# The convolution product of an attention layer: eight block products or seven

## The chip, the cores and the metric

The kernel runs on one core of one Trainium2 chip. The metric is the device time of one launch in microseconds (us), the median of several runs. The engines of the core run side by side, each through its own list of instructions in order: TensorE (PE; its weight loads are PEld), VectorE (DVE), ScalarE (ACT), GpSimd (POOL), and SyncE (SP), which here issues nearly all DMA transfers.

## The reference

One layer over 1024 latent tokens and 256 context tokens, model width 1024: a half-step SwiGLU network, then two token mixers side by side (a gated short convolution and an attention with 8 query heads and 2 key/value heads), merged by sigmoid gates, then a second SwiGLU network. What matters here is the mixing:

```python
y_conv_l = conv_branch(bg_l, cg_l, vc_l, conv_w[layer])          # (1024 tokens, 1024 channels)
o_l = latent_attention(q_l, k_all, v_all)
x = x + ml[5] * merge_branches(y_conv_l, o_l, gt_l, w_branch_conv[layer], w_branch_attn[layer], w_out[layer])

def merge_branches(y_conv, o_attn, gate_logits, w_bc, w_ba, w_out):
    g_conv, g_attn = jnp.split(jax.nn.sigmoid(gate_logits), 2, axis=-1)
    return (g_conv * (y_conv @ w_bc) + g_attn * (o_attn @ w_ba)) @ w_out
```

The change concerns `y_conv @ w_bc`, a product of 1024 x 1024 by 1024 x 1024, and its gate.

## The kernel before

All matmuls of weight carry precision in two parts: a float32 value is split into a high part (rounded to the matmul's format by ScalarE, `CAST`) and a low part (the difference, by VectorE or GpSimd, `TENSOR_TENSOR`). `split` (line 197) does it. A product of two values is then three matmuls: high by high, high by low, low by high (`mm3`). Latents lie with channels on the 128 partitions, so y is 8 blocks k of 128 channels by 1024 tokens, and the tokens are two chunks of 512, C0 and C1. y waits in DRAM (`yd`), the gates too (`gcd`), and the gated result goes to `zd`.

**The product with y.** `conv_inputs(ch)` (line 1523) loads the 8 blocks of a chunk and splits them. `conv_weights(j)` (line 1515) loads the 1024 x 128 columns of w_bc for output block j (512 KB, tile `raw`, 3 buffers) and splits them into `wc`. `conv_out(ch, j)` (line 1543) runs 8 x 3 = 24 matmuls of 512 columns into a PSUM bank, multiplies by the gate on VectorE (`g<-g,ps`) and stores to `zd`. That is 8 blocks x 2 chunks x 24 = 384 matmuls; each weight block is loaded and split twice.

**The attention.** There are 16 units (8 heads x 2 chunks), class `Unit` (line 1579). A unit has four query tiles; `scores` runs, for each, nine matmuls (three of 256 columns on `kc`, six of 512 on `kl`), VectorE takes the maxima (`m<-ps`, `nm`), and ScalarE the exponentials (`pc`, `pl`). The unit after it, `seconds` (line 1648) turns the previous unit's probabilities: ten steps of four transposes (`pt<-ident,pl`), a split on ScalarE and VectorE (`pts`), and three value matmuls (into `po` or `ps`). In the middle of it, `inverse` (line 1635) has VectorE take a reciprocal (`rinv`), and GpSimd's own DMA queue writes it to DRAM (`rinvd`) and reads it back spread over the partitions (`rrow`); GpSimd then scales the unit's output (`q<-q,rrow`).

**What sets the order.** Four products of C0 stand around the last head unit (its normalised, rotated heads are the tiles `xb`; `hsw` is a GpSimd helper of them; the transposes are `pt<-ident,xb`) and around unit 0's scores. The rest is in `fillers` (line 1705), a generator that the loop over units (line 1724) advances ten steps a unit: in most steps three matmuls of a block product stand in TensorE's list among the attention's. A scheduler then sets each engine's list from the program's order, its own estimates and the free tile slots; only instructions marked as pinned keep their written order. Short-lived 128 x 512 tiles all share 11 slots (`ttile`, line 116).

Of the kernel before, what the change touches and what calls it, by code (L numbers as in the profile page):

```python
# [9 lines left out]
F32 = mybir.dt.float32  # L10
F32R = mybir.dt.float32r
# [7 lines left out]
P = 128  # L19
D = 1024  # L20
KD = D // P
# [17 lines left out]
W_BUFS = 4  # L39
# [8 lines left out]
SLOT = 1024  # L48
# [3 lines left out]
def tile_dit_layer(  # L52
# [70 lines left out]
    def ps_s(n=512):  # L123
        return psum.tile([P, 512], F32, tag="s", name=uniq("ps"), bufs=5)[:, :n]
# [72 lines left out]
    def split(src, hi, lo, lo_eng=None, hi_eng=None):  # L197

        if hi_eng is dve:
            dve.tensor_copy(out=hi, in_=src)  # L200
        else:
            act.copy(out=hi, in_=src)
        (lo_eng or dve).tensor_sub(out=lo, in0=src, in1=hi.bitcast(F32))

    def load_parts(name, src, pinned=False):

        t = atile(name, (P, 2, 512), F32R)
        raw = t[:, 1].bitcast(F32)
        load(raw, src, pinned)
        split(raw, t[:, 0], t[:, 1])  # L210
        return t
# [280 lines left out]
    class Winograd:  # L492
# [21 lines left out]
        def keep(self, i, k, src, lo_eng=None):  # L514

            t = atile(f"r{i}", (P, 2, 512), F32R)
            split(src, t[:, 0], t[:, 1], lo_eng)
            self.r[i][k] = t
# [992 lines left out]
                )  # L1511

    ys, w_conv = {}, {}

    def conv_weights(j, lo_eng=None, tags=("wl", "wl")):
        raw = wpool.tile([P, SLOT], F32, tag="raw", name=uniq("raw"), bufs=3)
        hi, lo = (wpool.tile([P, SLOT], F32R, tag=tag, name=uniq("wc"), bufs=W_BUFS) for tag in tags)
        v = lambda t: t[:].rearrange("p (k n) -> p k n", k=KD)
        load(v(raw), w_bc[0][:, j * P : (j + 1) * P].rearrange("(k p) n -> p k n", p=P))
        split(raw[:], hi[:], lo[:], lo_eng)  # L1520
        w_conv[j] = v(hi), v(lo)

    def conv_inputs(ch, ks=range(KD), pinned=True):
        ys.setdefault(ch, []).extend(load_parts("y", yd[k, :, ch[1] : ch[1] + 512], pinned=pinned) for k in ks)

    before, N_UNITS = iter(()), 13
    for i, h in enumerate(heads()):
        run(before, 1)
        if i == N_UNITS - 1:
            conv_inputs(C0)  # L1530
        run(h, 1)
        if i == 0:
            for k in range(4):
                mix.part_second(k)
        if i == N_UNITS - 1:
            for j in range(2):
                conv_weights(j, tags=("wh", "wl"))
        run(before)
        before = h
    run(before, 1)  # L1540
    run(late_steps)

    def conv_out(ch, j):

        w, o = w_conv.pop(j), ch[1]
        ps, g = ps_s(), ttile("g")
        sp.dma_start(out=g, in_=gcd[j, :, o : o + 512])
        terms = [(w[0][:, k], w[1][:, k], ys[ch][k][:, 0], ys[ch][k][:, 1]) for k in range(KD)]
        for k in range(KD - 1):
            mm3(ps, terms, k, k + 1)  # L1550
            yield
        mm3(ps, terms, KD - 1)
        dve.tensor_mul(out=g, in0=g, in1=ps)
        sp.dma_start(out=zd[j, :, o : o + 512], in_=g)
        yield

    run(conv_out(C0, 0))
    conv_weights(2)
    run(before)
    run(conv_out(C0, 1))  # L1560
    conv_weights(3)

    o_parts = [None] * NQ

# [129 lines left out]
    u = units[0]  # L1697
    u.begin()
    for qt in range(4):
        u.scores(qt)  # L1700
        if qt < 3:
            run(conv_out(C0, 2 + qt))
            conv_weights(4 + qt)

    def fillers():

        for j in range(5, KD):
            conv_weights((j + 2) % KD, pool)
            yield from conv_out(C0, j)
            yield  # L1710
        for ks in ((0, 1), (2, 3), (4, 5), (6, 7)):
            conv_inputs(C1, ks, pinned=False)
            yield
            yield
        for j in range(KD):
            if j < KD - 2:
                conv_weights(j + 2, pool)
            yield from conv_out(C1, j)
            yield

    rest, fill = seconds(), fillers()
# [190 lines left out]
```

## Time and profile before

| | |
|---|---|
| median of 3 runs | 2631.08 us (2630.84 to 2632.65) |
| span of the profiled execution, its own time | 2631.1 us |
| TensorE busy | 2609.9 us (99%) |
| VectorE, ScalarE, GpSimd busy | 76%, 45%, 21% |
| granted TensorE clock, mean | 0.998 |
| matmuls that read y | 384, from 1415.9 to 1693.6 us |
| attention (scores to last value matmul) | 1427.7 to 1820.4 us |

A row of the timeline gives start, duration, engine, operation, out<-in, shapes, a count where neighbours are merged, and in brackets the idle time of the engine before it and what ended it. A row of a group gives count, then busy time and mean duration, then the idle time before such instructions. The time of a matmul's record is modelled and overlaps the next, so how many stand in a stretch says more than how long each is.

### The profile page before, as it was taken

Reading aid. Unit: us, or ns where it says so; the run is one execution under the profiler, and the core shown is the slowest. Engines: PE = TensorE matmul, PEld = TensorE weight load, DVE = VectorE, ACT = ScalarE, POOL = GpSimd, SP = SyncE. Lnnn points to the kernel's source line nnn. Section 1 sums busy time; section 2 is a strip of 40 time slices with the busy share of each in tenths; the row PEclk is TensorE's granted clock in tenths of the full one; section 3 lists DMA queues with packets and bytes.
Section 4 is the critical chain, followed back from the end, with each engine's and each line's share of the span. In section 5 each row is a group of like instructions: output and inputs, shape, how many; then the busy total and the mean of one; then the engine's idle time right before and its main releaser. Section 6 shows DMA issues by size and latency. Waiting matters only on the chain.

```text
span 2631.1 us, 35379 instructions
## 1 busy us (share of the span) xinstructions
PE 2609.9 (99%) x12665; PEld 2176.1 (83%) x12665; DVE 1997.4 (76%) x3360; ACT 1183.5 (45%) x2343; POOL 545.8 (21%) x425
## 2 busy tenths in 40 slices
PE   8999999999999999999999999999999999999998
PEld 5888899888888888888888888888888888888888
DVE  5888976877897879977788576676457886667996
ACT  6533454333454642333355566574237333334553
POOL 0133201221010034333022112132000442321100
PEclk9999999999999999999999999999999999999999
DMA  8665465345973365542522322113425653227831
GB/s 324 205 210 182 149 215 173 106 131 185 327 184 117 124 205 160 163 134 89 200 77 85 86 87 65 33 37 118 158 85 176 201 167 96 90 80 286 191 84 65
DMA packets 372905, 384.69 MB, mean 146 GB/s; under 512 B 19686, under 2 KB 256376, under 8 KB 372728
## 3 DMA queue, kind: packets, MB, share of 16 engines
q1 hardware_dynamic: 363288, 363.52, 42.1%
q0 software_dynamic: 9440, 18.91, 4.3%
q8 instruction: 99, 1.62, 0.2%
q14 instruction: 78, 0.64, 0.1%
HBM read 310.45 MB, written 71.86 MB: 145 GB/s over the span
## 4 chain that ended last, share of the span: by engine, by line
PE 94%; DVE 3%; DMA 1%; ACT 1%; issue 1%; SPq 0%; DVEq 0%; ACTq 0%
PE ps L90 81%; PE pt L90 8%; PE po L90 6%; DMA rawm<-in_w_mod_dram 1%; DVE xb L90 0%; DVE wl L90 0%; DVE macc L90 0%; DVE m L90 0%; DVE y L90 0%; DVE pts L90 0%; DMA xtok<-in_x_dram 0%; DVE x L90 0%; DVE r L90 0%; SPq L90 0%; DVE rs_t L90 0%
## 5 line engine op out<-in xcount | busy, mean ns | idle before, releaser
L90 PE MATMUL ps<-r,wl 128*128 128x512 f32 x5196 | 1198.3, 390 | 3.6 <-ACT r L90 1.3
L90 PEld LDWEIGHTS ps<-r,wl 128*128 128x128 f32 x5196 | 972.4, 188 | 207.7 <-ACT r L90 1.6
L90 ACT CAST wl<-sum 128x512 fp32r<-128x512 f32 x218 | 134.1, 622 | 294.4 <-PE ps L90 227.1
L90 ACT CAST wl<-raw 128x512 fp32r<-128x512 f32 x287 | 178.2, 622 | 193.1 <-PE ps L90 147.9
L90 DVE TENSOR_TENSOR wl<-raw,wl 128x512 fp32r<-128x512 f32 x287 | 210.2, 736 | 61.0 <-ACT wl L90 59.3
L90 DVE TENSOR_TENSOR wl<-sum,wl 128x512 fp32r<-128x512 f32 x218 | 196.9, 904 | 33.5 <-ACT wl L90 32.3
L90 POOL TENSOR_TENSOR sum<-raw 128x512 f32<-128x512 f32 x55 | 76.4, 1389 | 680.6 <-DMA raw<-in_ffn_w_in_dram 345.3
L90 DVE SCALAR_TENSOR_TENSOR macc<-rawm,silu_c,macc 128x512 f32<-128x512 f32 x178 | 145.4, 835 | 17.1 <-DMA rawm<-in_w_mod_dram 16.6
L90 DVE TENSOR_TENSOR u<-u,ps 128x512 f32<-128x512 f32 x186 | 126.5, 680 | 32.2 <-PE ps L90 32.1
L90 ACT CAST rh<-hid 128x512 fp32r<-128x512 f32 x132 | 82.2, 623 | 139.4 <-PE ps L90 112.3
L90 POOL TENSOR_TENSOR sum<-raw,sum 128x512 f32<-128x512 f32 x55 | 76.7, 1395 | 287.0 <-DVE wl L90 284.0
L90 DVE TENSOR_TENSOR pts<-pt,pts 128x512 fp32r<-128x512 f32 x160 | 107.3, 686 | 36.2 <-ACT pts L90 34.6
L90 DVE TENSOR_REDUCE m<-ps 128x1 f32<-128x256 f32 (+1 forms) x192 | 111.0, 597 | 29.4 <-PE ps L90 28.5
L90 ACT CAST pts<-pt 128x512 fp32r<-128x512 f32 x160 | 92.2, 597 | 85.5 <-PE pt L90 84.4
L90 PE MATMUL ps<-rh,wl 128*128 128x512 f32 x360 | 122.8, 390 | 0.0
L90 PE MATMUL ps<-wh,r 128*128 128x512 f32 x384 | 120.7, 392 | 0.0
L90 DVE TENSOR_TENSOR rl<-hid,rh 128x512 fp32r<-128x512 f32 x132 | 91.0, 693 | 29.9 <-ACT rh L90 19.4
L90 ACT CAST wh<-raw 128x512 fp32r<-128x512 f32 (+1 forms) x85 | 68.2, 803 | 95.5 <-PE ps L90 74.9
L90 PE MATMUL ps<-kl,qs 128*128 128x512 f32 x384 | 104.0, 394 | 0.1
L90 PE MATMUL ps<-rh,wh 128*128 128x512 f32 x300 | 102.8, 389 | 0.0
L90 PE MATMUL ps<-y,wc 128*128 128x512 f32 x384 | 95.3, 391 | 0.2 <-DVE g L90 0.2
L90 POOL TENSOR_TENSOR sum<-sum,raw 128x512 f32<-128x512 f32 x55 | 87.8, 1597 | 5.7 <-PE ps L90 3.9
(325 smaller groups left out, 5102.3 us busy)
## 6 DMA issues: line engine op xcount, KB each, us to landing
raw<-in_ffn_w_in_dram SPq DMA_DIRECT2D x131, 512.0 KB
raw<-in_ffn_w_out_dram SPq DMA_DIRECT2D x72, 512.0 KB
raw<-in_w_in_dram SPq DMA_DIRECT2D x64, 512.0 KB
rawm<-in_w_mod_dram SPq DMA_DIRECT2D x104, 256.0 KB
hid<-hd SPq DMA_DIRECT2D x40, 512.0 KB
ucd<-uc SPq DMA_DIRECT2D x33, 512.0 KB
rawm<-in_w_mod_dram SPq DMA_DIRECT2D x32, 512.0 KB
ws<-in_ffn_w_out_dram POOLq DMA_DIRECT2D x26, 512.0 KB, 6.4
```

Of the source, the lines that this page charges most:

```text
L90: inst = getattr(self.engine, name)(*args, **kw)
```

## The change

The product is taken as blocks of two by two: y in halves of channels and halves of tokens, w_bc in halves of inputs and of outputs. Seven products of half blocks (4 x 3 matmuls into each output block of 128) stand for eight. They run in four groups, `GROUPS = ((1, 2), (7, 6), (5, 4), (3,))`, and each group over p = 0 to 3, the output block within a half. Running sums u and v go to DRAM between groups (`uvd`) and come back.

- Group 0 (products 1 and 2) uses y as it is: u is product 1 (a copy by ScalarE), and product 1 plus 2, summed in PSUM, is the lower half of the outputs for C0.
- Groups 1 and 2 need sums of blocks of y and of w_bc. Blocks of y are loaded into the shared 512-wide tiles (`yb`), summed on VectorE, split by ScalarE and GpSimd. Sums of weights are made on GpSimd in the `raw` tiles.
- Group 3 needs one block of y as it is, and sums of weights.
- Each block product ends in additions on VectorE and, where an output is complete, its gate on VectorE, from SBUF (`uv<-uv,g`).

`conv_sums` loads the raw weights two pairs ahead and sums them, `conv_weights` splits them one pair ahead, `conv_inputs` is now a generator with steps of its own, and `fillers` runs groups 1 to 3.

```diff
-    def conv_weights(j, lo_eng=None, tags=("wl", "wl")):
-        raw = wpool.tile([P, SLOT], F32, tag="raw", name=uniq("raw"), bufs=3)
...
-    def conv_inputs(ch, ks=range(KD), pinned=True):
-        ys.setdefault(ch, []).extend(load_parts("y", yd[k, :, ch[1] : ch[1] + 512], pinned=pinned) for k in ks)
+    uvd = [dram.tile([2, P, 512], F32, name=uniq("uvd")) for _ in range(4)]
+    GROUPS = ((1, 2), (7, 6), (5, 4), (3,))
+    conv_order = [(g, p) for g in range(4) for p in range(4)]
+    w_raw = {}
+
+    def conv_sums(at):
...
+        if g == 0:
+            t, _, _ = raw(p)
+        elif g == 1:
+            (t, s3, a0), (_, b0, b1) = raw(p, 0, 4, 512), raw(p + 4)
+            pool.tensor_sub(out=s3, in0=a0, in1=b0)
+            pool.tensor_add(out=b0, in0=b0, in1=b1)
+            pool.tensor_sub(out=a0, in0=b0, in1=a0)
+        elif g == 2:
+            t, b0, b1 = raw(p + 4)
+            pool.tensor_add(out=b0, in0=b0, in1=b1)
+        else:
+            (t, a0, a1), (b, _, _) = raw(p), raw(p + 4)
+            pool.tensor_sub(out=t[:], in0=t[:], in1=b[:])
+            pool.tensor_add(out=a0, in0=a0, in1=a1)
+        w_raw[g, p] = t
...
+    def conv_inputs(g, pinned=False):
+
+        def keep(i, k, src):
+            t = ys[i, k] = atile("y", (P, 2, 512), F32R)
+            split(src, t[:, 0], t[:, 1], pool)
...
+        ts = fetch(0)
+        for k in range(4):
+            for _ in range(3):
+                yield
+            b22, b12, b11 = ts[:3]
+            if g == 1:
+                dve.tensor_sub(out=b12, in0=b22, in1=b12)
+                dve.tensor_add(out=b11, in0=b11, in1=b12)
+                keep(7, k, b12)
+                keep(6, k, b11)
+            else:
+                dve.tensor_sub(out=b12, in0=b12, in1=b11)
+                dve.tensor_sub(out=b22, in0=b22, in1=ts[3])
+                dve.tensor_sub(out=b22, in0=b22, in1=b12)
...
+            if k < 3:
+                ts = fetch(k + 1)
...
+        elif g == 2:
+            u, v, gc = kept(0), kept(1), gate(p + 4, C0)
+            yield from blocks(4, ps, 4)
+            b = ttile("uv")
+            dve.tensor_sub(out=b, in0=v, in1=ps)
+            dve.tensor_mul(out=b, in0=b, in1=gc)
+            result(p + 4, C0, b)
+            yield
+            ps, gc = ps_s(), gate(p + 4, C1)
+            yield from blocks(5, ps, 0)
+            dve.tensor_add(out=v, in0=v, in1=ps)
+            dve.tensor_add(out=u, in0=u, in1=ps)
+            keep(u, 0)
+            dve.tensor_mul(out=v, in0=v, in1=gc)
+            result(p + 4, C1, v)
...
-        for j in range(5, KD):
-            conv_weights((j + 2) % KD, pool)
-            yield from conv_out(C0, j)
-            yield
...
+        for n, (g, p) in enumerate(conv_order[4:], 4):
+            if p == 0:
+                yield from conv_inputs(g)
+            conv_weights(n + 1, pool)
+            for i, _ in enumerate(conv_pair(g, p)):
+                if i == 2:
+                    conv_sums(n + 2)
+                yield
             yield
```

How the change moves instructions, at two places. First TensorE, between the last two head units and unit 0's first scores (`ps<-y,wc` is a block product, `pt<-ident,xb` a transpose of a head, `kc` and `kl` the keys, `qs` unit 0's split queries, its second operand tile being the low part). Before:

```order
L90 MATMUL ps_13172<-y_13000,wc_13076 128x512 x2
L90 MATMUL ps_13172<-y_13000,wc_13077 128x512
L90 MATMUL ps_13213<-kc_11559,qs_13207 128x256 x2
L90 MATMUL ps_13222<-kl_11555,qs_13207 128x512
L90 MATMUL ps_13222<-kl_11556,qs_13207 128x512
L90 MATMUL ps_13227<-kl_11557,qs_13207 128x512
L90 MATMUL ps_13227<-kl_11558,qs_13207 128x512
L90 MATMUL ps_13213<-kc_11559,qs_13208 128x256
L90 MATMUL ps_13222<-kl_11555,qs_13208 128x512
L90 MATMUL ps_13227<-kl_11557,qs_13208 128x512
L90 MATMUL pt_13160<-ident,xb_13031 128x128
L90 MATMUL ps_13237<-y_12972,wc_13155 128x512 x2
```

Now, at the same place:

```order
L90 MATMUL ps_13179<-y_12990,wc_13081 128x512 x2
L90 MATMUL pt_13158<-ident,xb_13035 128x128
L90 MATMUL ps_13211<-kc_11559,qs_13205 128x256 x2
L90 MATMUL ps_13211<-kc_11559,qs_13206 128x256
L90 MATMUL ps_13220<-kl_11555,qs_13205 128x512
L90 MATMUL pt_13158<-ident,xb_13066 128x128
L90 MATMUL pt_13158<-ident,xb_13035 128x128
L90 MATMUL pt_13158<-ident,xb_13066 128x128
L90 MATMUL pt_13164<-ident,xb_13035 128x128
```

The first transpose of the last head unit has come ahead of the scores, the low part of the queries is read by the third score matmul instead of the eighth, and the other transposes follow after four scores instead of after nine and 12 more block products.

Second GpSimd, from the last `hsw` of the head units on (`rinvd` and `rrow` are unit 0's, then the next unit's). Before:

```order
L90 DMA rinvd_13606<-rinv_13604 128x4x1
L90 DMA rrow_13608<-rinvd_13606 128x512
L90 TENSOR_TENSOR wc_13414<-raw_13412,wc_13413 128x1024
L90 DMA rinvd_13872<-rinv_13870 128x4x1
L90 TENSOR_TENSOR wc_13612<-raw_13610,wc_13611 128x1024
L90 DMA rrow_13874<-rinvd_13872 128x512
L90 TENSOR_TENSOR q_12156<-q_12156,rrow_13608 128x512
```

Now:

```order
L90 TENSOR_TENSOR raw_13267<-raw_13267 128x512
L90 TENSOR_TENSOR raw_13265<-raw_13267,raw_13265 128x512
L90 DMA rinvd_13592<-rinv_13590 128x4x1
L90 DMA rrow_13594<-rinvd_13592 128x512
L90 TENSOR_TENSOR y_13461<-yb_13401,y_13461 128x512
L90 TENSOR_TENSOR y_13464<-yb_13403,y_13464 128x512
L90 TENSOR_TENSOR y_13521<-yb_13469,y_13521 128x512
L90 TENSOR_TENSOR y_13524<-yb_13471,y_13524 128x512
L90 TENSOR_TENSOR y_13598<-yb_13529,y_13598 128x512
L90 TENSOR_TENSOR y_13601<-yb_13531,y_13601 128x512
L90 DMA rinvd_13871<-rinv_13869 128x4x1
L90 TENSOR_TENSOR y_13709<-yb_13606,y_13709 128x512
```

The eight low parts of the sums of y for products 7 and 6 stand behind unit 0's `rinvd` and `rrow`, the last two of them behind the next unit's `rinvd` as well. The first block product of group 1 reads `y_13464`, `y_13524` and `y_13601` in that order.

More of the change, by code (lines that the diff above doesn't have):

```diff
@@ new lines, in conv_weights, with y_block @@
+    def conv_weights(at, lo_eng=None, tags=("wl", "wl")):
+        if at >= len(conv_order):
+            return
+        g, p = conv_order[at]
+        n, t = 512 * len(GROUPS[g]), w_raw.pop((g, p))
+        hi, lo = (wpool.tile([P, SLOT], F32R, tag=tag, name=uniq("wc"), bufs=W_BUFS)[:, :n] for tag in tags)
+        split(t[:, :n], hi, lo, lo_eng)
+        w_conv[g, p] = [v.rearrange("p (k n) -> p k n", n=P) for v in (hi, lo)]
+    def y_block(k, lower, right):
+        return yd[k + 4 * lower, :, 512 * right : 512 * right + 512]
@@ L1535, in tile_dit_layer @@
         if i == N_UNITS - 1:
-            for j in range(2):
-                conv_weights(j, tags=("wh", "wl"))
+            for p in range(2):
+                conv_sums(p)
+                conv_weights(p, tags=("wh", "wl"))
         run(before)
@@ L1557, in tile_dit_layer, with conv_pair, blocks, kept @@
-    run(conv_out(C0, 0))
-    conv_weights(2)
+    def conv_pair(g, p):
+        w = w_conv.pop((g, p))
+        def blocks(i, ps, at, begins=True):
+            for k in range(4):
+                wh, wl = (v[:, at + k] for v in w)
+                y = ys[i, k]
+                matmul(ps, wh, y[:, 0], start=begins and k == 0, stop=False, on=not begins)
+                matmul(ps, wh, y[:, 1], start=False, stop=False, on=not begins)
+                matmul(ps, wl, y[:, 0], start=False, stop=k == 3, on=not begins)
+                if k < 3:
+                    yield
+        def kept(v):
+            t = ttile("uv")
+            sp.dma_start(out=t, in_=uvd[p][v])
+            return t
+        def keep(t, v):
+            sp.dma_start(out=uvd[p][v], in_=t)
+        def gate(j, ch):
+            t = ttile("g")
+            sp.dma_start(out=t, in_=gcd[j, :, ch[1] : ch[1] + 512])
+            return t
+        def result(j, ch, t):
+            sp.dma_start(out=zd[j, :, ch[1] : ch[1] + 512], in_=t)
+        ps = ps_s()
+        if g == 0:
+            gc, u = gate(p, C0), ttile("uv")
+            yield from blocks(1, ps, 0)
+            act.copy(out=u, in_=ps)
+            keep(u, 0)
+            yield
+            yield from blocks(2, ps, 4, False)
+            dve.tensor_mul(out=gc, in0=gc, in1=ps)
+            result(p, C0, gc)
+        elif g == 1:
+            u, t = kept(0), ttile("uv")
+            yield from blocks(6, ps, 4)
+            dve.tensor_add(out=t, in0=u, in1=ps)
+            keep(t, 0)
+            yield
+            yield from blocks(7, ps, 0, False)
+            dve.tensor_add(out=u, in0=u, in1=ps)
+            keep(u, 1)
+        elif g == 2:
[5 more added lines that the diff above has]
+            result(p + 4, C0, b)
+            yield
+            ps, gc = ps_s(), gate(p + 4, C1)
+            yield from blocks(5, ps, 0)
+            dve.tensor_add(out=v, in0=v, in1=ps)
+            dve.tensor_add(out=u, in0=u, in1=ps)
+            keep(u, 0)
+            dve.tensor_mul(out=v, in0=v, in1=gc)
+            result(p + 4, C1, v)
+        else:
+            u, gc = kept(0), gate(p, C1)
+            yield from blocks(3, ps, 0)
+            dve.tensor_add(out=u, in0=u, in1=ps)
+            dve.tensor_mul(out=u, in0=u, in1=gc)
+            result(p, C1, u)
+        yield
@@ L1559, in tile_dit_layer, with conv_begin @@
+    def conv_begin():
+        for p in range(4):
+            if p:
+                conv_weights(p + 1)
+            for i, _ in enumerate(conv_pair(0, p)):
+                if i == 3:
+                    conv_sums(p + 2)
+                yield
+    begin = conv_begin()
+    run(begin, 7)
     run(before)
-    run(conv_out(C0, 1))
-    conv_weights(3)
+    run(begin, 7)
     o_parts = [None] * NQ
@@ L1701, in tile_dit_layer @@
         if qt < 3:
[L1702 to L1703 removed]
+            run(begin, 6)
+    run(begin)
     def fillers():
[L1707 to L1718 removed]
+        for n, (g, p) in enumerate(conv_order[4:], 4):
[5 more added lines that the diff above has]
+                    conv_sums(n + 2)
+                yield
             yield
```

46 lines of the change are left out of this document (30 added, 16 removed).

## The prediction

> **What bounds the kernel now.** I read the page first (busy times, then the chain that ended last), then the waits of TensorE, then the busy times by stretch in the part that the change touches.
>
> ```profile
> span 2631.1 us, 35379 instructions
> PE 2609.9 (99%) x12665; PEld 2176.1 (83%) x12665; DVE 1997.4 (76%) x3360; ACT 1183.5 (45%) x2343; POOL 545.8 (21%) x425
> PE 94%; DVE 3%; DMA 1%; ACT 1%; issue 1%; SPq 0%; DVEq 0%; ACTq 0%
> ```
>
> TensorE is busy 99% of the span and holds 94% of the chain. So a matmul taken out is worth its whole slot, as long as nothing that TensorE waits for gets later. The span (2631.1) and the median of the three runs (2631.08) are the same number, so sums against the one are sums against the other. The three runs spread over 1.8 us; about 0.2% (5.3 us) is what a measurement of this kernel can tell from no change, so "faster" means below 2625.8 here.
>
> The order of the instructions is the same in both kernels up to the first product with y (1415.9 us) and again from the branch merges on (about 1820 us). Everything happens in between. The next rows give that part by stretches: core time, then busy time (and count) of each engine.
>
> ```profile
> core 0: us, PE busy (x) PEld busy (x) DVE busy (x) ACT busy (x) POOL busy (x), PEclk, DMA share, GB/s
> 1416.00:1456.00 40.00, 39.80 (x192) 32.98 (x191) 29.23 (x58) 17.63 (x42) 4.38 (x5) 1.00 0.41 132
> 1506.00:1545.00 39.00, 38.22 (x211) 31.67 (x209) 30.41 (x66) 29.10 (x72) 9.54 (x8) 1.00 0.33 101
> 1545.00:1694.00 149.00, 148.62 (x803) 124.36 (x802) 93.41 (x203) 87.97 (x223) 27.83 (x23) 1.00 0.19 54
> 1694.00:1744.00 50.00, 49.52 (x286) 41.75 (x284) 37.43 (x83) 35.24 (x93) 6.10 (x7) 1.00 0.09 22
> sum 374.00, PE 370.83 PEld 309.80 DVE 256.04 ACT 234.04 POOL 83.74; mean PE 46.35 PEld 38.72 DVE 32.01 ACT 29.25 POOL 10.47
> ```
>
> The last row sums eight stretches from 1416 to 1790 us. TensorE is idle 3.2 us of 374 there; VectorE is busy 68%. The third row is attention mixed with convolution products (idle 0.38 of 149 us, VectorE at 63%). The fourth is attention alone, after the fillers have run out (idle 0.48 of 50, VectorE at 75%). The second holds the 8 splits of y for the second chunk, which bring no matmul (idle 0.78 of 39, VectorE at 78%). So TensorE stays the bound in all of them, and its idle share goes up with VectorE's load: 0.3%, 1.0%, 2.0%.
>
> **The change, part by part.**
>
> *48 matmuls go.* Seven block products of 48 matmuls stand where eight stood: 336 instead of 384.
>
> ```profile
> 1438.02 5.61 PE L90 MATMUL ps<-y,wc 128*128 128x512 f32 x24
> L90 PE MATMUL ps<-y,wc 128*128 128x512 f32 x384 | 95.3, 391 | 0.2 <-DVE g L90 0.2
> ```
>
> The mean of 391 ns is one matmul's record, and records overlap: 24 in a row take 5.61 us from the first start to the last end, so starts are (5.61 - 0.39) / 23 = 0.227 us apart. 48 x 0.227 = **10.9 us less**. By the group's union (95.3 / 384 = 0.248, too high, since the ends of short rows stand out) it would be 11.9. I take 10.9.
>
> *The start of the products moves against the last head unit.* TensorE's rows there are shown with the change: before, 23 products and nine score matmuls stand between the eight transposes of one head unit and the first of the next; now 23 products alone, then a transpose, four scores, and the other seven transposes.
>
> ```profile
> 1422.40 5.48 PE L90 MATMUL ps<-y,wc 128*128 128x512 f32 x23
> 1426.32 1.22 DVE L90 TENSOR_TENSOR qs<-q,qs 128x512 fp32r<-128x512 f32 x1
> 1427.46 1.22 DVE L90 TENSOR_TENSOR xb<-xb,hsw 128x512 f32<-128x512 f32 x1
> 1427.71 0.40 PE L90 MATMUL ps<-kc,qs 128*128 128x256 f32 x2
> 1429.81 0.68 DVE L90 TENSOR_TENSOR xb<-xb,hsw 128x512 f32<-128x512 f32 x1
> 1429.94 3.00 PE L90 MATMUL ps<-y,wc 128*128 128x512 f32 x12 [0.20 <-DVE g L90]
> 1432.78 0.93 PE L90 MATMUL pt<-ident,xb 128*128 128x128 f32 x7
> 1436.97 0.52 PE L90 MATMUL ps<-kc,qs 128*128 128x256 f32 x3
> ```
>
> VectorE is fixed by its own chain up to here. It now does the first xb addition ahead of qs: xb by about 1427.5, qs by 1428.7, the second xb by 1430.0 (the last of these 0.4 us earlier than before). TensorE ends its 23 products near 1427.5, transposes, does two scores, waits about 0.9 us for qs, does two more and waits about 0.9 for the second xb. Against some 0.6 lost there before (0.2 shows at 1429.94, and a gap shows only beyond the 0.16 by which a record outlasts its slot): **+1.2 us**; from -0.5 (even the old wait goes) to +3 (it also waits for the first xb).
>
> *GpSimd's queue ahead of group 1.* The sums of y for products 7 and 6 are split by GpSimd, and in its order (shown with the change) six of these subtractions stand behind rinvd and rrow of unit 0.
>
> ```profile
> 1599.03 0.80 POOL L90 DMA_DIRECT2D rinvd<-rinv  x1 [10.31 <-DVE rinv L90]
> 1608.10 0.56 POOL L90 DMA_DIRECT2D rrow<-rinvd  x1 [8.27 <-DMA rinvd<-rinv]
> 1608.67 1.30 POOL L90 TENSOR_TENSOR q<-q,rrow 128x512 f32<-128x512 f32 x1
> ...
> DMA to landing us min/median/max: 8.0/8.6/12.1
> ...
> POOL rrow L90 <- DMA rinvd<-rinv: 94.3, 12, 9.7
> ```
>
> These are GpSimd's rows in order of time for one unit, then the landing of rinvd over all 16 units, and the wait of rrow in this part of the program (total, times, longest). The queue stands 9.1 us between the issue of rinvd and that of rrow, until the first has landed. Before, only a weight split or a product's scaling stood behind that, needed late. Now, counted from unit 0's reciprocal, the sixth subtraction ends at 9.1 + 0.6 + 6 x 1.3 = 17.5 us. Behind the score matmuls that stand beside that reciprocal, TensorE's order has 20 matmuls of 512 columns and 10 of 256 for scores, 24 transposes, 19 value products and 8 block products up to the one that reads the sixth result. A 256-column matmul takes (0.52 - 0.28) / 2 = 0.12 and a transpose (0.93 - 0.28) / 6 = 0.11 (the rows at 1436.97 and 1432.78), so that is 47 x 0.227 + 10 x 0.12 + 24 x 0.11 = 14.5 us. **+2.8 us**, a little under the difference of 3.0, since TensorE loses some of it earlier anyway; from 0 (it comes later for other reasons) to +6 (the landing takes 12.1).
>
> *More work on VectorE, ScalarE and GpSimd.* The groups of instructions (count | busy, mean ns | idle before) that price it:
>
> ```profile
> L90 DVE TENSOR_TENSOR u<-u,ps 128x512 f32<-128x512 f32 x186 | 126.5, 680 | 32.2 <-PE ps L90 32.1
> L90 DVE TENSOR_TENSOR u<-u,v 128x512 f32<-128x512 f32 x50 | 51.3, 1025 | 3.4 <-ACT u L90 2.4
> L90 DVE TENSOR_TENSOR g<-g,ps 128x512 f32<-128x512 f32 x16 | 11.0, 686 | 11.4 <-PE ps L90 11.3
> L90 DVE TENSOR_TENSOR wc<-raw,wc 128x1024 fp32r<-128x1024 f32 x7 | 9.1, 1295 | 0.5 <-ACT wc L90 0.5
> L90 ACT CAST y<-y 128x512 fp32r<-128x512 f32 x16 | 9.3, 640 | 0.0
> L90 POOL TENSOR_TENSOR wc<-raw,wc 128x1024 fp32r<-128x1024 f32 x9 | 21.6, 2400 | 10.3 <-ACT wc L90 10.2
> L90 POOL TENSOR_TENSOR sum<-raw,sum 128x512 f32<-128x512 f32 x55 | 76.7, 1395 | 287.0 <-DVE wl L90 284.0 <-DVE rs_a L90 3.0
> ```
>
> VectorE had 16 splits of y, 16 gate products and 7 weight splits. It gets 8 splits, 20 sums of y, 28 operations on a PSUM result (24 additions or subtractions, 4 gate products), 12 gate products from SBUF and 5 weight splits: 36 more of 0.69 us less two of 1.3, **+22 us of work**, 278 of some 365 us, or 76% instead of 68%. ScalarE gets 12 more splits of y (0.64 each), four copies and four half-wide weight casts for whole ones: +8 us, 66%. GpSimd gets 20 splits of y (1.3 each), 20 weight sums of 512 columns (1.4) and four of 1024, and fewer whole weight splits: about +65 us, 40%. None is full on average; all of it lies beside TensorE, and costs what the idle share rises by. From 63% to about 75% VectorE load that share goes from 0.3% to 1.0% in the rows above: over the 150 us that were mixed, 1.1 us, and the steps without matmuls (32 in the fillers instead of 8) add a little, while the stretch of attention alone at the end gets shorter. **+1.3 us**, from 0 to +6.
>
> The upper end is the two SBUF inputs. u<-u,v and u<-u,ps are the same operation on the same shape; the first reads both inputs from SBUF, and takes 1025 ns against 680. The 20 sums and 12 gate products of the change are of the first kind: 32 x 0.34 = 11 us more on VectorE if they meet GpSimd as often as those do, 79% instead of 76%. [...]
>
> *Moves that I cost at nothing.* SP issues 8 more weight loads, 24 more of y, and 32 for u and v: 64 x 0.4 us of a queue that waits most of the time, and 11 MB more at a DMA share of 0.09 to 0.41. What hides it is the distance: raw weights are fetched two pairs ahead, with 24 products and some 18 us of attention between pairs. If that cover goes, a pair stalls for as long as its load is late (the last rival).
>
> Sum: -10.9 + 1.2 + 2.8 + 1.3 = -5.6: **2631.1 - 5.6 = 2625.5 us**.
>
> **The rivals.**
>
> *Nothing is given back.* The gain arrives whole: 2631.1 - 10.9 = 2620.2. For it: TensorE's waits in this part are a handful, 0.8 us at most, and attention alone still runs at 99%. Against it: the queue of GpSimd above, which this needs to be no wait.
>
> *VectorE is full in places.* Between the last gate product of group 0 and the first addition of group 1, VectorE's order has 57 operations: 23 maxima at 0.597 (their mean in the trace), 16 of 0.69 for attention and y, one qs split and 17 small ones, some 28 us; TensorE's order has 25.5 us there. If the five sums in it cost 1.03 instead of 0.69 and all of the surplus comes through, it is +2.5 + 1.7 = 4.2, and about as much again in the sums for products 5 and 4, which are 12 in as many filler steps: -10.9 + 1.2 + 2.8 + 6 = -0.9, **2630.2 us**, no change. For it: the idle share at 78%. Against it: neighbours overlap (two splits in 1.29 us), and the stretch with y before, 78% too, lost only 0.8 us. [...]
>
> *Loads that queue behind stores.* Each pair of groups 1 to 3 stores u or v and loads them again; SP issues in order, and a store waits for VectorE, which waits for TensorE. The loads of u, v and gates for group 2 stand behind the last four blocks of y, whose tiles GpSimd has to free. VectorE's subtraction on such a u stands in order ahead of the maxima of the next scores, so TensorE would follow. In the trace stores of this stage hold SP up to 22 us:
>
> ```profile
> SPq L90 <- DVE g L90: 150.4, 12, 22.2
> ```
>
> It decides once u is later than its product: from there each microsecond counts, in eight pairs (groups 2 and 3). At 1.5 us each it is 12 on top: 2625.5 + 12 = **2637 us**, slower. Against it: the loads are written ahead of the products, and no wait of VectorE for a gate load shows now.
>
> **How the numbers follow.** Forecast, 2625.5 with its own range of 2622.5 to 2628.5: 0.50, of which 0.31 lies below 2625.8. All of it arrives (2620.2): 0.17. VectorE full in places (2630.2): 0.24. Loads behind stores (2637): 0.09. So faster 0.31 + 0.17 = 0.48, same 0.19 + 0.24 = 0.43, slower 0.09. The range leaves the slow case out and the outer tails of the second and third: **2619 to 2632**.
>
> **What would show it.** Matmuls with y: 336, starts 0.227 apart. First 23 products, then TensorE waiting for VectorE's qs and xb, 1.8 us in all. In unit 1, TensorE waiting for GpSimd's y, about 3 us, with rrow's wait ahead of it; if that wait is missing, the second rival's sum is nearer. [...] Waits of VectorE for uv or g loads would be the slow case. I am wrong if TensorE loses more than 8 us or less than 2 us to the new work, or if something moves outside 1415 to 1820 us.

## The result and the profile after

| | median, us | range, us | ratio to the kernel before, 95% interval |
|---|---|---|---|
| before, run beside it | 2631.42 | 2630.84 to 2632.65 | |
| changed | 2679.85 | 2678.24 to 2680.92 | 1.018 (1.0166 to 1.0195) |

The changed kernel is 48 us slower, where 5.6 us faster was forecast. It lies far outside the range (2619 to 2632), and on the side to which only the last rival pointed. The profiled execution spans 2678.0 us, 46.9 more than that of before. First the page of the changed kernel (span, busy times, the chain by engine):

```profile
span 2678.0 us, 35544 instructions
PE 2613.8 (98%) x12617; PEld 2174.7 (81%) x12617; DVE 2029.9 (76%) x3394; ACT 1187.4 (44%) x2359; POOL 608.4 (23%) x471
...
PE 88%; DVE 4%; DMA 4%; issue 1%; ACT 1%; POOL 1%; SPq 0%; DVEq 0%; POOLq 0%; ACTq 0%
```

TensorE has 48 fewer matmuls and yet is busy 3.9 us longer, and transfers (DMA) have 4% of the chain instead of 1%. Next the busy times by stretch, from the first product with y to the last score matmul, first of before, then of the changed kernel. The columns are: length, then busy time and count of TensorE, its weight loads, VectorE, ScalarE and GpSimd, then granted clock, share of the DMA engines, GB/s.

```profile
1415.90:1788.00 372.10, 369.00 (x2000) 308.40 (x1999) 254.52 (x550) 232.91 (x591) 81.84 (x78) 1.00 0.24 67
```

```profile
1415.90:1836.00 420.10, 374.51 (x1963) 308.35 (x1963) 284.44 (x587) 240.86 (x609) 143.96 (x124) 0.96 0.35 99
```

This stretch holds the whole difference (48.0 us). TensorE is idle 420.1 - 374.5 = 45.6 us in it, against 3.1 before: 42.5 more. Its busy time has risen by 5.5 although work was taken out, and the mean clock is 0.96 instead of 1.00: matmuls ran slowly for a while. So two things have to be explained, the idle time and the clock. The waits of TensorE in this part (total, times, longest) say what it stood for:

```profile
PE pt L90 <- DVE pts L90: 18.4, 8, 8.6
PE ps L90 <- ACT pts L90: 12.3, 5, 7.8
PE ps L90 <- ACT pc L90: 8.7, 5, 3.3
PE po L90 <- ACT pts L90: 3.8, 2, 3.3
PE ps L90 <- ACT uv L90: 1.2, 1, 1.2
...
PE ps L90 <- POOL y L90: 0.3, 1, 0.3
```

Hardly any of it is waiting for y or its products. TensorE waits for the attention's own splits (pts) of VectorE and ScalarE, 34.5 us in all and up to 8.6 us at a time, and 8.7 us for exponentials (pc); before, the splits were 1.9 us in all and pc 0.8. For the splits of y by GpSimd, which the forecast had priced at 2.8, it waits 0.3 us once. VectorE's waits in this part tell why most of pts was late. Before, VectorE waited for no transfer here; now there is one such row:

```profile
DVE yb L90 <- DMA yb<-yd: 27.0, 6, 9.8
```

A sum of two blocks of y whose load has not landed holds up the maxima and the splits that stand behind it in VectorE's list, and so the attention: the sum at 1471.87 us starts after 7.05 us of idleness that its load ended, the next maximum follows at 1473.87, the next split at 1475.06. The chain shows such loads (start, duration, what; rows of transfers from 1461 to 1603 us), and GpSimd's rows show when the reciprocals of a unit were stored:

```profile
1461.94 9.84 DMA yb<-yd
...
1555.62 2.59 DMA yb<-yd
...
1563.73 10.05 DMA uvd<-uv
1573.80 4.70 DMA yb<-yd
...
1591.11 2.54 DMA yb<-yd
...
1602.73 8.21 DMA yb<-yd
```

```profile
1457.83 0.84 POOL L90 DMA_DIRECT2D rinvd<-rinv  x1 [14.67 <-DVE rinv L90]
...
1562.17 0.78 POOL L90 DMA_DIRECT2D rinvd<-rinv  x1 [6.01 <-DVE rinv L90]
...
1598.14 0.78 POOL L90 DMA_DIRECT2D rinvd<-rinv  x1 [13.76 <-DVE rinv L90]
```

Read the two together. The transfers at 1555.62 and 1591.11, issued with no such store under way, take 2.5 to 2.6 us. Those at 1461.94, 1563.73 and 1602.73, issued 4.1, 1.6 and 4.6 us after a store of rinvd, take 9.8, 10.1 and 8.2. The one at 1573.80, issued 11.6 us after a store and only once the slow store of u had landed, takes 4.7; these two end the longest wait of VectorE, 9.8 us. A store of rinvd writes 2 KB, as 512 pieces of 4 bytes (row `rinvd` seen from 128 partitions, 4 values each). It lands in 7.7 to 10.8 us here, and it is in the kernel before as well, with much the same landing (8.0 to 12.1).

One of the long stalls, the 7.8 us up to 1728, comes about in another way. GpSimd's, SyncE's, ScalarE's and TensorE's rows there:

```profile
1716.46 0.56 POOL L90 DMA_DIRECT2D rrow<-rinvd  x1 [9.08 <-DMA rinvd<-rinv]
1717.04 1.31 POOL L90 TENSOR_TENSOR wc<-raw,wc 128x512 fp32r<-128x512 f32 x1
...
1718.37 0.38 SPq L90 DMA_DIRECT2D raw<-in_w_branch_conv_dram  x1
...
1720.12 2.23 SPq L90 DMA_DIRECT2D y<-yd  x4
...
1724.35 0.62 ACT L90 CAST y<-y 128x512 fp32r<-128x512 f32 x1 [7.56 <-DMA y<-yd]
...
1728.04 0.80 PE L90 MATMUL ps<-pts,vh 128*128 128x512 f32 x1 [7.80 <-ACT pts L90]
```

GpSimd stands 9.08 us for the landing of rinvd and only then splits a weight; SyncE waits 8.1 us for that split, since its next load overwrites the raw weight; the four blocks of y for product 3 stand behind that load in SyncE's order; ScalarE stands 7.56 us for the first of them, ahead of the pts that TensorE needs. Issued 8.1 us earlier, these blocks would have landed at about the time at which ScalarE came to them (an estimate from these rows). So here the same store acts chiefly through GpSimd's queue; the loads of y themselves take 4 to 5 us.

Last the clock, around this stall (same columns as above):

```profile
1712.00:1720.00 8.00, 8.00 (x48) 6.65 (x46) 5.67 (x13) 3.56 (x10) 3.11 (x3) 1.00 0.34 41
1720.00:1728.00 8.00, 0.23 (x2) 0.00 (x0) 0.00 (x0) 2.97 (x6) 4.78 (x3) 0.79 0.90 282
1728.00:1730.00 2.00, 1.96 (x8) 1.78 (x9) 1.07 (x3) 2.00 (x7) 2.00 (x3) 0.50 0.92 330
1730.00:1732.00 2.00, 2.00 (x8) 1.62 (x7) 0.80 (x3) 0.85 (x2) 1.76 (x2) 0.63 0.01 2
1732.00:1734.00 2.00, 2.00 (x16) 1.73 (x15) 1.85 (x5) 0.73 (x2) 0.00 (x0) 1.00 0.37 125
```

After 7.8 us of idleness TensorE comes back with a granted clock of 0.50: in 2 us it begins 8 matmuls, then 8, and 16 once the clock is at 1.00 again. So this stall costs its own length and nearly 2 us more. Shorter gaps brought it too (0.60 after 2.7 us in f3_b16, last section). The kernel before, whose longest gap here was 0.8 us, has nothing of it: its clock is 1.00 over the whole stretch.

### The profile page after: what moved, and what is told of

It is laid out like the page before. It is cut to its first block, busy times and chain, and to the rows that moved or that the text cites. A ratio compares the mean times of both kernels' runs of the same rounds, so it can differ in the third digit from the quotient of the medians.

```text
span 2678.0 us, 35544 instructions
## 1 busy us (share of the span) xinstructions
PE 2613.8 (98%) x12617; PEld 2174.7 (81%) x12617; DVE 2029.9 (76%) x3394; ACT 1187.4 (44%) x2359; POOL 608.4 (23%) x471
## 2 busy tenths in 40 slices
DMA packets 387242, 402.53 MB, mean 150 GB/s; under 512 B 20710, under 2 KB 263544, under 8 KB 387064
## 4 chain that ended last, share of the span: by engine, by line
PE 88%; DVE 4%; DMA 4%; issue 1%; ACT 1%; POOL 1%; SPq 0%; DVEq 0%; POOLq 0%; ACTq 0%
PE ps L90 76%; PE pt L90 7%; PE po L90 5%; DMA yb<-yd 1%; DMA raw<-in_w_branch_conv_dram 1%; DMA rawm<-in_w_mod_dram 1%; POOL raw L90 1%; DVE m L90 0%; DVE wl L90 0%; DVE xb L90 0%; DMA rinvd<-rinv 0%; DVE macc L90 0%; DMA uvd<-uv 0%; DVE pts L90 0%; ACT x L90 0%
## 5 line engine op out<-in xcount | busy, mean ns | idle before, releaser
L90 DVE SCALAR_TENSOR_TENSOR macc<-rawm,silu_c,macc 128x512 f32<-128x512 f32 x178 | 146.6, 842 | 14.8 <-DMA rawm<-in_w_mod_dram 14.4
L90 DVE TENSOR_REDUCE m<-ps 128x1 f32<-128x512 f32 (+1 forms) x192 | 110.4, 595 | 28.3 <-PE ps L90 27.0
L90 POOL DMA_DIRECT2D ws<-in_ffn_w_out_dram x30 | 35.6, 1235 | 255.9 <-PE ps L90 115.0
L90 PE MATMUL pt<-ident,pl 128*128 128x128 f32 x512 | 79.7, 279 | 10.4 <-DVE pts L90 9.4
```

Source lines behind the costliest of these rows:

```text
L90: inst = getattr(self.engine, name)(*args, **kw)
```

## The experiments

Theory A: VectorE stands in order behind y blocks that land late, and TensorE behind VectorE. Rival B: with the added sums VectorE is simply too full. Inside A, either the store of rinvd slows the loads (A1), or they are issued late for want of a free tile (A2).

**e1_noload: no loads of yb.**

```diff
-                ts.append(ttile("yb"))
-                load(ts[-1], y_block(k, *at))
+                ts.append(k_lat[at[0]][at[1]][:, 0].bitcast(F32))
...
```

Each sum reads parts of the keys instead and goes to a new tile, so what comes out is not the product any more.

> The changed kernel without the 28 loads of yb: the sums for products 7, 6, 5, 4 read parts of the latent keys, which lie in SBUF, and write new tiles; their sums, splits and products are done as before, with other numbers. Theory A (VectorE stands in order behind y blocks that land late, and TensorE behind VectorE): the 27.0 us of VectorE's waits for yb go, and with them TensorE's gaps before 1470.8, 1474.6, 1580.5 and 1615.5 (3.3 + 3.3 + 8.6 + 7.7) and about 6 us of half clock after them: 2680 - 29 = about 2651. [...]

Measured: 2686.59 us, ratio 1.0202 (1.0187 to 1.0218), no gain at all. By the numbers that is rival B, which had above 2672, but the waits say otherwise. First VectorE's and then GpSimd's in this part of the run:

```profile
DVE yb L90 <- POOL y L90: 11.9, 2, 6.0
DVE yb L90 <- DMA uvd<-uv: 6.5, 1, 6.5
DVE qs L90 <- DMA zd<-uv: 5.3, 1, 5.3
```

```profile
POOL rrow L90 <- DMA rinvd<-rinv: 86.7, 10, 10.5
```

VectorE stands 23.7 us at the sums and at qs, nearly as long as for the loads, now for a free tile to write to: GpSimd, which has to read the tile that stood there, waits for rinvd, or a store out of it (u, z) has not landed. So the loads of yb were not the cause but one of several things that were late at the same moments. Theory A as put, with the loads at fault, falls; what all of them may share is the store of rinvd, which the next runs try.

**e2_rows: the store in 4 pieces of 512 bytes.**

```diff
-            rinv = small("rinv", 4)
-            dve.reciprocal(out=rinv[:], in_=self.rsum[:])
+            pr = ps_s()[:4, :P]
+            transpose(pr, self.rsum[:])
+            rinv = ttile("rinv", P)[:4]
+            dve.reciprocal(out=rinv, in_=pr)
...
-            pool.dma_start(out=row.rearrange("(j p) -> p j", p=P), in_=rinv[:])
+            pool.dma_start(out=row.rearrange("(j p) -> j p", p=P), in_=rinv)
```

> The changed kernel, with the reciprocals turned by TensorE into 4 rows of 128 before they are stored: rinvd is written as 4 rows of 512 bytes instead of 512 pieces of 4 bytes (one more 128x4 transpose per unit). Theory A1 (y blocks are late because they are issued while a rinvd store of 4-byte pieces is under way, which slows every transfer for some 10 us): rinvd lands in 2 to 4 us instead of 9, the loads of yb and y land in 2 to 3 us, and the time falls to 2645 to 2660. Rival A2 (y blocks are late because SP issues them late, having waited for one of 11 shared tiles): 2670 to 2685.

Measured: 2641.64 us, ratio 1.0031 (1.0019 to 1.0043): 38 us of the 48 are gone, a little more than A1 had said (2645 to 2660). VectorE's waits for yb fall to 3.3 us. But the edit also moves instructions (GpSimd takes four splits of y ahead of the store), so a run without that was still needed (e5_16b).

**e3_late: the store as it was, rrow read five steps later**, so that GpSimd stands behind it less.

```diff
-            self.rows = ttile("rrow")
-            pool.dma_start(out=self.rows, in_=row.partition_broadcast(P))
+            self.row = row
...
             act.copy(out=of, in_=self.po)
-            pool.tensor_mul(out=of, in0=of, in1=self.rows)
+            rows = ttile("rrow")
+            pool.dma_start(out=rows, in_=self.row.partition_broadcast(P))
+            pool.tensor_mul(out=of, in0=of, in1=rows)
```

> The changed kernel with rrow's load issued in output(), five steps after the store of rinvd, so that GpSimd seldom stands waiting for that store; the store itself is as before. Theory A1: the store still slows the loads, 2665 to 2685. Rival A2 in the form that GpSimd's wait for rinvd holds up its splits of y and so the tiles that the next loads need: VectorE's waits for yb fall below 10 us and the time to 2655 or less.

Measured: 2674.76 us, ratio 1.016 (1.0145 to 1.0175). That is 5 us less, and the intervals overlap. But the edit took only part of GpSimd's wait away, as its rows show (the changed kernel, then this run):

```profile
POOL rrow L90 <- DMA rinvd<-rinv: 80.3, 11, 9.1
```

```profile
POOL rrow L90 <- DMA rinvd<-rinv: 49.6, 6, 10.7
```

VectorE still waits 15.0 us for yb, 11.3 for stores of z and 8.1 for GpSimd. So this run does not price the blocked queue, and how the loss divides between it and the slow transfers stays open.

**e4_lead: twice the lead for the loads, the store as it was.**

```diff
-            for _ in range(3):
+            for _ in range(6):
                 yield
```

> The changed kernel with six steps instead of three between the fetch of a row of y blocks and their sums, in groups 1 and 2 (24 more steps in which the attention goes on without a product; the attention alone at the end gets shorter by as much). Theory A, whatever makes the loads late: a lead of some 10 us instead of 5 covers most of it, VectorE's waits for yb fall from 27 to under 8 us, 2650 to 2660. Rival B: unchanged or slower, above 2672.

Measured: 2709.29 us, ratio 1.0288 (1.0271 to 1.0305), 29 us slower still. The waits for yb halve (12.5 us), but VectorE now stands 18.3 us for tiles of qs that GpSimd has not read out, and the products' last steps run beside the end of the last unit. This run decides little; it suggests that lead is of no use while the tiles themselves are held.

**e5_16b: the store in 128 pieces of 16 bytes.** The order of instructions is the same as in the changed kernel on all five engines. Only the scales come back in another order and meet other queries.

```diff
-            pool.dma_start(out=row.rearrange("(j p) -> p j", p=P), in_=rinv[:])
+            pool.dma_start(out=row.rearrange("(p j) -> p j", p=P), in_=rinv[:])
```

> The changed kernel with rinvd written as 128 pieces of 16 bytes instead of 512 pieces of 4 (in another order, so the scales meet other queries). Theory A1 (it is the number of pieces that makes the store slow, and the store that makes loads late): rinvd lands in 3 to 5 us, and the time falls most of the way to e2_rows, 2640 to 2655. Rival (e2_rows gained by its other order of instructions, or by the store coming from 4 partitions): landing above 7 us and 2670 or more.

Measured: 2647.73 us, ratio 1.0058 (1.0043 to 1.0073). The landing of rinvd over the 16 units (minimum, median, maximum), first of the changed kernel, then of this one:

```profile
DMA to landing us min/median/max: 7.7/9.2/10.8
```

```profile
DMA to landing us min/median/max: 1.7/1.8/2.8
```

With nothing else changed, 1.018 - 1.0058 = 1.2% of 2632, some **32 us, hang on the pieces of this one store**. That is shown. How they divide is not: GpSimd's wait for the landing falls too, from 80.3 to 14.8 us. Nor is it shown how the store holds up other transfers.

**b1_rows and f3_b16: does the store cost the kernel before anything?** They are the kernel before with the edit of e2_rows, and with that of f1_16 (below).

> The kernel before, with the reciprocals stored as 4 rows of 512 bytes as in e2_rows. Theory A (the slow store is in the kernel before too, but its loads are issued so far ahead that nothing waits for them): within 3 us of before, the 16 more transposes (16 x 0.11) against a little less waiting. Rival (the store costs the kernel before as much per unit, so e2_rows gained something that has nothing to do with the change): 5 us or more faster than before.

> The kernel before with the same two edits as f1_16. Theory: nothing waits for the store there, so within 3 us of before, and the 8 us that b1_rows lost came from its transposes in TensorE's order, not from the store. Rival (the slow store costs the kernel before too, and b1_rows hid that gain): 2626 or less.

Measured: 2641.04 us, ratio 1.0032 (1.0019 to 1.0045), and 2636.20 us, ratio 1.0012 (1.0003 to 1.0021). Neither gains: the slow store was covered in the kernel before. Both lose. For f3_b16 that is a little more than the theory's 3 us, for b1_rows 8.7 us, which the theory did not have. For b1_rows one price is plain, the reciprocal of 4x128 takes 934 ns on VectorE, that of 128x4 took 178; what makes the rest stays open. The loss of f3_b16 is one stall, and the most telling one of this study. VectorE's row at that place, first before, then in f3_b16:

```profile
1460.52 0.69 DVE L90 TENSOR_TENSOR qs<-q,qs 128x512 fp32r<-128x512 f32 x1
```

```profile
1460.02 3.12 DVE L90 TENSOR_TENSOR qs<-q,qs 128x512 fp32r<-128x512 f32 x1
```

And GpSimd's rows there, before and in f3_b16:

```profile
1469.05 0.58 POOL L90 DMA_DIRECT2D rrow<-rinvd  x1 [10.49 <-PE pt L90]
1469.65 2.41 POOL L90 TENSOR_TENSOR wc<-raw,wc 128x1024 fp32r<-128x1024 f32 x1
```

```profile
1459.59 0.58 POOL L90 DMA_DIRECT2D rrow<-rinvd  x1 [1.82 <-PE pt L90]
1460.19 2.39 POOL L90 TENSOR_TENSOR wc<-raw,wc 128x1024 fp32r<-128x1024 f32 x1
```

The store lands sooner, so GpSimd comes to its weight split 9.5 us sooner, and starts 0.17 us after VectorE starts the low part of qs, whose two inputs both lie in SBUF. VectorE's instruction lasts 3.12 instead of 0.69 us, to 0.56 us past the end of GpSimd's 2.39. By these records the one that starts first is the one held. TensorE waits 2.7 us for the pts behind it, and its clock is 0.60 over the 3.6 us that follow.

**b2_48: what 48 matmuls are worth alone**, in the kernel before. It leaves out the last of the eight blocks of every product; loads and splits stay.

```diff
         for k in range(KD - 1):
-            mm3(ps, terms, k, k + 1)
+            mm3(ps, terms[: KD - 1], k, k + 1)
             yield
-        mm3(ps, terms, KD - 1)
```

> The kernel before with 48 of its 384 matmuls with y left out (the last of the 8 blocks of each of the 16 products; loads and splits stay). Theory: a slot is worth 0.227 us and nothing follows, so 10.9 us less than before. Rival (TensorE follows VectorE or the loads already): 5 us less or nothing.

Measured: 2623.91 us, ratio 0.9969 (0.9958 to 0.998): 8.4 us less, the interval reaching from 5 to 11. So the removed matmuls are worth about what was taken for them, less a little: TensorE's waits come to 5.0 us here, against 3.5 before.

**f1_16: the fast store, with every scale at its query.** GpSimd reads the scales with a stride.

```diff
-            pool.tensor_mul(out=of, in0=of, in1=self.rows)
+            of4, rows4 = of.rearrange("q (j p) -> q j p", j=4), self.rows.rearrange("q (p j) -> q j p", j=4)
+            pool.tensor_mul(out=of4, in0=of4, in1=rows4)
```

> The changed kernel with rinvd written as 128 pieces of 16 bytes, and the scales read with a stride by GpSimd's multiplication, so that every query meets its own. Theory A1: as e5_16b, 2642 to 2650, if the strided read costs GpSimd no more than 1.3 us per unit. Rival (the strided read takes several us and holds GpSimd's queue up again): 2655 or more.

Measured: 2650.37 us, ratio 1.0067 (1.0054 to 1.008), beside e5_16b's 1.0058. The strided multiplication takes 1612 ns against 1306. From here on the question is what is left, 18 us against the kernel before.

**f4_pool: the sums of y on GpSimd** (f1_16, and the five operations of `conv_inputs` on `pool` instead of `dve`).

> f1_16 with the 20 sums of y on GpSimd instead of VectorE. [...] Rival (GpSimd, with 28 us more, delivers the splits of y late, and TensorE waits for y): 2650 or more.

Measured: 2636.07 us, ratio 1.0009 (1.0 to 1.0017), 0.58% or 15 us less than f1_16, at the lower end of what its theory had (2636 to 2643). One large stall is left. TensorE's longest wait here, then VectorE's row and GpSimd's rows at that place:

```profile
PE ps L90 <- DVE qs L90: 5.1, 1, 5.1
```

```profile
1466.62 6.64 DVE L90 TENSOR_TENSOR qs<-q,qs 128x512 fp32r<-128x512 f32 x1 [0.77 <-POOL yb L90]
```

```profile
1465.30 1.29 POOL L90 TENSOR_TENSOR yb<-yb,yb 128x512 f32<-128x512 f32 x1
1466.55 1.27 POOL L90 TENSOR_TENSOR y<-yb,y 128x512 fp32r<-128x512 f32 x1
1467.79 1.26 POOL L90 TENSOR_TENSOR yb<-yb,yb 128x512 f32<-128x512 f32 x1
1469.02 3.69 POOL L90 TENSOR_TENSOR y<-yb,y 128x512 fp32r<-128x512 f32 x3
```

One subtraction that takes 0.69 us alone lasts 6.64, from inside GpSimd's run to 0.55 us after the run's last instruction ended (1469.02 + 3.69 = 1472.71). It ended after all five instructions of GpSimd that follow one another there without a pause, not after the first of them.

**f5_poolA: f4_pool, with unit 0's exponentials written to other tiles.**

```diff
-            if self.hd == 0 and self.ch[1] == 0 and qt < 2:
+            if self.hd == 0 and self.ch[1] == 0 and qt < 0:
```

> f4_pool, with unit 0's first two tiles pl in the 1024-wide shared tiles of the other units instead of the tiles of raw weights, so that unit 0's exponentials no longer wait for GpSimd's weight sums (ScalarE waited 2.0 + 1.3 us there, TensorE 2.7, and its clock was at half for 3.4 us after). Theory: 3 to 5 us less than f4_pool. Rival (TensorE then waits for yb or the next unit's qs at the same place): within 1.5 us of f4_pool.

Measured: 2641.15 us, ratio 1.0029 (1.0017 to 1.0041), 5 us slower. TensorE's waits for exponentials fall from 1.8 to 0.7 us, but it now waits at three new places around the last head's transposes, 2.5 us in all, and 6.0 us before unit 2's scores. That last wait is again for the subtraction of qs, behind seven instructions of GpSimd now, the last of which ends at 1480.27:

```profile
1472.34 8.48 DVE L90 TENSOR_TENSOR qs<-q,qs 128x512 fp32r<-128x512 f32 x1
```

So the gain was lost to the same kind of wait, which neither the theory nor the rival had as 5 us slower.

**e7_ra4: e2_rows with four steps of lead.**

> e2_rows with four steps instead of three between the fetch of y blocks and their sums. Theory: what e2_rows still loses to the kernel without waits (some 17 us) lies in units 0 to 2 and 6, where sums of yb are made, and is for a good part VectorE waiting for yb; with 2 us more lead 2632 to 2638. Rival (the 11 shared tiles, held longer, set the pace): 2642 or more.

Measured: 2641.39 us, ratio 1.0033 (1.0022 to 1.0045), the same as e2_rows, and so nearer the rival (2642 or more) than the theory. Behind the fast store, lead alone gains nothing as long as VectorE makes the sums.

**g2_qs, g3_lo and g4_qs4: GpSimd's runs or late loads?** g2_qs is f4_pool with the low part of qs on GpSimd in units 1 to 11. g3_lo is f1_16 with the low parts of the sums of y on VectorE. g4_qs4 is g2_qs with four steps of lead.

```diff
-            split(q_of(self.hd, self.ch), *self.qs)
+            split(q_of(self.hd, self.ch), *self.qs, pool if 0 < units.index(self) < 12 else None)
```

> f4_pool with the subtraction that makes the low part of qs, in units 1 to 11, on GpSimd instead of VectorE. Theory P (VectorE's operations with two SBUF inputs stand behind GpSimd's back-to-back instructions): the 6.64 us instruction and TensorE's gap of 5.1 us before unit 2's scores go, with 1.7 us of half clock: 2627 to 2631. Rival L (something else is late there too: GpSimd delivers qs no earlier, in its own order): 2634 to 2640.

> f1_16 with the 16 subtractions that make the low parts of the sums of y on VectorE, like the sums, instead of GpSimd; VectorE has 11 us more to do. Theory P: no GpSimd run is left to stand behind in the stage of sums, the 20 sums take about 0.7 us each instead of 0.97, the longest qs subtraction falls from 4.8 to under 1.5 us, and the time to 2640 to 2646. Rival (VectorE's amount of work decides): 2652 or more.

> g2_qs with four steps instead of three between the fetch of y blocks and their sums. Theory P: GpSimd's runs are already out of the way, so within 2 us of g2_qs. Rival L (loads of yb still set the pace): 3 us or more faster than g2_qs.

Measured: g2_qs 2629.68 us, ratio 0.9991 (0.9982 to 1.0); g3_lo 2642.62, ratio 1.0042 (1.0029 to 1.0055); g4_qs4 2625.23, ratio 0.9972 (0.9962 to 0.9982). The times of g2_qs and g3_lo are as theory P had them. Not all of the rest is: in g2_qs the gap of 5.1 us before unit 2's scores has shrunk to 2.3, now a wait for qs from GpSimd; in g3_lo the sums take 765 ns, but the longest qs subtraction is still 2.8 us. g4_qs4 is 4.5 us faster than g2_qs, as rival L had it; GpSimd's waits for loads of yb fall from 15.2 to 6.6 us, and the gap of 2.3 us is gone. So both seem to be there: first GpSimd's runs, then, once these are out of VectorE's way, the loads. g4_qs4 beats both kernels. Its stretch from first product to last score, and its page's busy times:

```profile
1416.40:1781.00 364.60, 359.35 (x1946) 298.55 (x1945) 260.81 (x551) 238.69 (x604) 187.79 (x159) 1.00 0.39 118
```

```profile
PE 2601.4 (99%) x12617; PEld 2166.2 (83%) x12617; DVE 2003.1 (76%) x3363; ACT 1188.0 (45%) x2359; POOL 647.3 (25%) x502
```

TensorE is idle 5.3 us there, the clock is at 1.00, and GpSimd, not VectorE, carries the new work (187.8 us, before 81.8).

## Why the prediction was wrong

Its steps in order.

- **48 matmuls, -10.9.** Held, near the edge: b2_48 gave 8.4 less, the interval reaching to 11.
- **The start, +1.2.** The size held by luck, the reason did not. TensorE waits 1.22 us once, for ScalarE's copy of u: product 2 adds into the PSUM bank that this copy is still reading, and the 23 products start late. For xb it waits 0.2 us, for qs not at all.
- **GpSimd's queue, +2.8.** GpSimd does stand about 9 us behind rinvd, as the rows had said, but TensorE waits for its y only 0.3 us. The damage takes another way, through tiles that GpSimd has not read out and that loads or sums then lack: in the 7.8 us stall above it goes by a weight tile, SyncE's order and a late load of y. How much of the loss it makes no run shows; e3_late, which took some 31 of the 80 us of waiting away, gained about 5 us.
- **More work on VectorE, +1.3 (0 to +6).** Too small, and beyond its upper end. By the mean share VectorE was never full: 68% of the stretch in the changed kernel (284.4 of 420.1), as before (254.5 of 372.1). But with the fast store in place, moving the sums off it gained 15 us (f1_16 to f4_pool), moving qs as well 5 more. Two things were in that: sums stand in order behind their loads (10.0 us of VectorE's waits in f1_16), and instructions with two SBUF inputs stand behind GpSimd (4.83 us instead of 0.69 for a subtraction of qs there). g3_lo, which takes only the low parts of the sums of y from GpSimd, gains 7.8 although VectorE then does more; that speaks for the second as about half of the 15, but VectorE's waits for the loads fall there as well (10.0 to 6.7 us), so the two are not cleanly divided. The forecast had a row for it (u<-u,v at 1025 ns against 680) and turned it into 0.34 us for each of 32 operations. In the trace of before that row holds two kinds: 31 of the 50 have no instruction of GpSimd beside them and take 687 ns on average, 19 have one and take 1577; u<-u,ps, with one input in PSUM, takes 679 and 682. The sums indeed took 908 ns on average, 15 of them 688 with GpSimd idle and 5 of them 1567 beside it:

```profile
L90 DVE TENSOR_TENSOR yb<-yb,yb 128x512 f32<-128x512 f32 x20 | 18.1, 908 | 27.1 <-DMA yb<-yd 27.0
```

  The mean lies within what was foreseen (0.69 to 1.03) and is cheap. What costs is the single instruction of 3 to 8.5 us with the attention behind it, as in f3_b16, f1_16 (4.83), f4_pool and f5_poolA, and that a mean doesn't show. In the changed kernel itself the longest sum takes 1.94 us, and the longest of the new instructions, 3.35 us, holds TensorE up by less than 1 us.
- **Moves costed at nothing: here the forecast failed.** "What hides it is the distance: raw weights are fetched two pairs ahead." That is true of the weights and was let stand for the blocks of y, which are fetched three steps ahead of sums that VectorE does in order. The second half of the error is that a landing time was taken as a property of a load. The prediction had the row that 2 KB of rinvd land in 8.0 to 12.1 us, and used it for GpSimd's queue alone; it never asked what else is under way in those 9 us, sixteen times. e5_16b shows the price, some 32 us of the 48. (The 11 MB named there are a slip: 64 transfers of 256 KB and more are at least 16.8 MB, and the pages of the two kernels, 402.53 and 384.69 MB, differ by 17.8. No step of the sum rests on it.)
- **The rivals.** "Loads that queue behind stores" had the sign and the kind (VectorE, then TensorE, behind a late load), but it named the loads of u, and took 1.5 us for a stall. SP's order, which it named too, does play its part in the 7.8 us stall. It was given 0.09, because no wait of VectorE for such a load shows in the trace before; of the new loads, which had no cover, that trace could show nothing.
- **Left out altogether: the clock.** A stall of TensorE was priced at its length. The stretch holds 42.5 us more idle time, and 5.5 more busy time where some 9 less were due (48 matmuls are 10.9, of which TensorE's order puts some beyond this stretch): around 14 us, by this estimate, came from the half clock and ragged restarts.

## What to carry to other kernels

Before moving a load close to its use, look up what is in flight at that moment on every queue: a store in 4-byte pieces cost nothing while all loads had slack (b1_rows, f3_b16), and cost 32 us once some had none (e5_16b), so write such rows in larger pieces first. Put new work that waits for transfers (VectorE stood 27.0 us for yb), or that lasts longer beside GpSimd (the sums: 1.57 us instead of 0.69), on an engine that nobody waits for, even if each operation takes twice as long there (the sums: 1.3 us on GpSimd, 0.7 to 0.9 on VectorE, and 15 us faster in all). And count a stall of TensorE of more than 2 us as its length plus almost 2 us: from the first product with y on, the half clock came with 43 of the 47 such gaps in the traces of all these runs, in the changed kernel with all 7 of them (2.2 to 8.6 us long), where its shortfall came to 1.6 to 2.2 us after each gap that had no other close behind it.

## What was not expected of the hardware

- 2 KB to DRAM: 512 pieces of 4 bytes land in 7.7 to 10.8 us, 128 pieces of 16 bytes in 1.7 to 2.8 (e5_16b; one of f1_16 took 5.7), 4 pieces of 512 bytes in 1.5 to 4.8, half of them within 1.6 (e2_rows). In the chain of the changed kernel three transfers of 256 KB issued while the first kind was under way took 8.2 to 10.1 us, two issued clear of it 2.5 to 2.6.
- A subtraction of qs on VectorE, with both inputs in SBUF, ended only after a whole run of GpSimd's instructions, not after the first of them: it took 8.48 us behind seven in a row, 6.64 behind five, 3.12 behind one of 2.39, alone 0.69. All three end 0.55 to 0.56 us after the last of GpSimd's.
- Making one engine faster can cost time: the faster store alone made the kernel before 4 us slower (ratio 1.0012, 1.0003 to 1.0021), since GpSimd's next instruction came to lie beside VectorE's, which took 3.12 us instead of 0.69.
- The half clock came after gaps of TensorE of only 2.0 to 2.7 us. After one of 2.0 us in f1_16 the clock was 0.58 over 4 us, and after one of 2.7 us in f3_b16 0.60 over the 3.6 us that follow; after one of 3.5 us, in e4_lead at 1649.0 us, it stayed at 1.00. So these traces show no length that decides it. The rows of f3_b16:

```profile
1460.00:1464.40 4.40, 1.76 (x8) 1.12 (x6) 4.38 (x4) 0.96 (x2) 2.56 (x2) 0.94 0.89 197
1464.40:1468.00 3.60, 3.52 (x14) 3.07 (x15) 2.48 (x5) 2.40 (x8) 0.00 (x0) 0.60 0.41 124
```
